# The beginning of a hybrid decoder step: modulation on four column tiles, square sums by a matrix of ones, three half weight tiles drawn forward

## The chip, the cores and the metric

One core of a Trainium2 chip. The metric is the device time of one launch in microseconds: 2328.43 us, the median of three runs (2324.95 to 2330.56). The profiled execution took 2327.78 us, of which 2326.1 us are the span that the profile shows.

## The reference

One layer of a decoder with two groups of heads beside each other, for a prompt of 2048 rows and for eight samples of four rows. Each row of width 1024 is normalised by its root mean square, scaled and shifted by a modulation that comes from a small vector `c`, and projected by one wide matrix. The projected columns feed a state-space group (Mamba-2, 16 heads) and a gated delta-rule group (8 heads), each behind a causal convolution of four taps; their outputs are joined, projected back, gated and added to the row.

```python
mod = jax.nn.silu(c.astype(f32)) @ w_ada.astype(f32) + b_ada.astype(f32)
shift, scale, gate = jnp.split(mod, 3, axis=-1)
h = _rmsnorm(x, norm_w) * (1.0 + scale[:, None]) + shift[:, None]
proj = h @ w_in.astype(f32)
z_s, xbc_raw, dt_raw, z_g, qkv_raw, a_raw, b_raw = _split(proj, IN_SIZES)
...
out = x.astype(f32) + gate[:, None] * (mix @ w_out.astype(f32))
```

The prompt and the eight samples have nine vectors `c`, so the modulation is a product of 9 rows with a 1024 x 3072 matrix.

## The kernel before

**Stages.** Stage one works on the prompt in four pieces of 512 rows. A piece's h is kept with the model dimension on partitions, as eight blocks (index k) of 128 x 512, split in a high and a low part (`hhi`, `hlo`); every product with `w_in` is three matmuls (high x high, low x high, high x low). Stage two, from 1859 us on, is the output projection. This study is about the beginning, in which the first piece's h is made.

**Making the first h.** `stat_first` (L290 to L303) loads the eight x blocks, squares each on ACT and sums the squares over partitions with matmuls against a column of ones, so that the sums stand with rows on partitions. `stat_row` takes the inverse root, writes it on a diagonal (L280) and spreads it over all partitions with a matmul by ones (L283). `h_load` multiplies x by it on DVE (L309); `h_make` applies scale and shift and casts to the high part on ACT (L313, L314) and forms the low part on DVE (L315).

**Modulation.** `ada_cols` (L161 to L175) makes 512 columns of the modulation, called a block here: four loads of 512 KB, eight fp32 matmuls of 9 x 512 (L168), a copy to SBUF (L170), four small matmuls that turn the rows into columns (L173, called the turn), and the bias on DVE (L174). There are two shift blocks and two scale blocks; blocks with index 0 serve k = 0 to 3, those with index 1 serve k = 4 to 7. `ada_gate` does the two blocks of the output gate at the end of stage one, two k at a time, in between other work (L195).

**The order.** PE's instructions stand as the Python code issues them. The code registers functions with a place `tau` (`at`) and runs them sorted by it; DVE, ACT, POOL and SP are ordered by a scheduler. Ahead of the sorted list run the first shift block, the square sums, the first scale block and the first four k of h. At `tau` 2.3 `second_half` runs the other two blocks and the other four k.

**Weight tiles.** A 128-column tile of `w_in` is used in two halves of four k, 12 matmuls each (L531), called first half and second half. `q0` opens a PSUM bank of the pool `ip` (three banks) and runs the first half, `q1` runs the second half and then the convolution of the result: a scaling on ACT (L536), three taps on DVE (L539, L545), a copy of the last columns on ACT (L547), a tanh on ACT (L548), a product on DVE (L549) that reads the bank last. `want` loads the halves ahead in the order of the list `halves` and splits them: a cast on ACT (L495), a subtraction on POOL (L496). Tiles 0, 1, 2, 3 below are the first four tiles.

**The decay gates.** `gates` multiplies h by a small matrix (L414, first for k = 0 to 3, then for k = 4 to 7), copies, turns it with four matmuls (L424), and `gate_set` computes softplus and decay on DVE and ACT (L343 to L366; the logarithm at L351 needs another function table of ACT than the tanh). Its last result `g_ln` goes to a cumulative sum on PE (L371, L372), and all heads need that.

## Time and profile before

| | |
|---|---|
| median of the runs | 2328.43 us |
| the profiled execution | 2327.78 us |
| its span | 2326.1 us |
| first matmul | 9.02 us |
| square sums end | 30.4 us |
| first matmul on h | 49.07 us |
| first matmul on the second half of h | 75.81 us |
| cumulative sum of the gates (L371) | 97.72 us |

A row of the timeline has the start in us, the duration in us, the engine, the line of the kernel, the operation with its output and inputs, the shapes, and how many instructions were merged (x4). In square brackets stands the idle time of the engine just before it and what released it. A matmul on plain fp32 leaves two records, one on the rounded fp32r type one. Rows of stretches give start:end, length, and the busy time of each engine with its number of instructions.

### The profile page before, as it was taken

Reading aid. Unit: us, or ns where it says so; the run is one execution under the profiler, and the core shown is the slowest. Engines: PE = TensorE matmul, PEld = TensorE weight load, DVE = VectorE, ACT = ScalarE, POOL = GpSimd, SP = SyncE. Lnnn points to the kernel's source line nnn. Section 1 sums busy time; section 2 is a strip of 40 time slices with the busy share of each in tenths; the row PEclk is TensorE's granted clock in tenths of the full one; section 3 lists DMA queues with packets and bytes.
Section 4 is the critical chain, followed back from the end, with each engine's and each line's share of the span. In section 5 each row is a group of like instructions: output and inputs, shape, how many; then the busy total and the mean of one; then the engine's idle time right before and its main releaser. Section 6 shows DMA issues by size and latency. Waiting matters only on the chain. (4 is left out here: it accounts for less than half of the span.)

```text
span 2326.1 us, 41856 instructions
## 1 busy us (share of the span) xinstructions
PE 2200.8 (95%) x15405; PEld 1864.9 (80%) x15405; DVE 1481.9 (64%) x3574; ACT 953.1 (41%) x2680; POOL 826.7 (36%) x1052
## 2 busy tenths in 40 slices
PE   6999999989999999999999989999999799998998
PEld 3688878868897887889788889998899377786786
DVE  2466868786767768675666776668676564454323
ACT  2534556454536445442533453435433432231111
POOL 3255665554437243411522241215211554322000
PEclk8999999999999999999999999999999999999999
DMA  6354655555766675465645544555445563643321
GB/s 239 113 167 152 191 166 180 181 181 174 225 214 209 213 225 183 143 193 165 191 153 179 178 135 132 180 154 157 150 147 160 165 211 125 191 155 128 129 86 52
DMA packets 241112, 387.94 MB, mean 167 GB/s; under 512 B 75880, under 2 KB 132968, under 8 KB 240908
## 3 DMA queue, kind: packets, MB, share of 16 engines
q1 hardware_dynamic: 240908, 385.28, 52.2%
q8 instruction: 121, 1.98, 0.3%
q14 instruction: 83, 0.68, 0.1%
HBM read 289.89 MB, written 95.30 MB: 166 GB/s over the span
## 5 line engine op out<-in xcount | busy, mean ns | idle before, releaser
L531 PE MATMUL pip<-hhi,w 128*128 128x512 f32 (+1 forms) x2880 | 823.7, 362 | 6.7 <-DVE kT L549 4.9
L531 PEld LDWEIGHTS pip<-hhi,w 128*128 128x128 f32 x2880 | 515.0, 190 | 85.0 <-issue 6.9
L531 PE MATMUL pip<-hlo,w 128*128 128x512 f32 (+1 forms) x1440 | 509.8, 354 | 0.0
L619 PE MATMUL pip<-w,hhi 128*128 128x256 f32 x2048 | 382.6, 287 | 0.3 <-DVE cv L549 0.3
L496 POOL TENSOR_TENSOR w<-xin,w 128x512 fp32r<-128x512 f32 x156 | 202.6, 1301 | 378.3 <-ACT w L495 344.8
L619 PEld LDWEIGHTS pip<-w,hhi 128*128 128x128 f32 x2048 | 316.5, 190 | 2.4 <-DVE cv L549 0.5
L531 PEld LDWEIGHTS pip<-hlo,w 128*128 128x128 f32 x1440 | 274.5, 191 | 36.9 <-issue 4.5
L619 PE MATMUL pip<-w,hlo 128*128 128x256 f32 x1024 | 289.4, 283 | 0.0
L1185 PE MATMUL pip<-wohi,mh 128*128 128x512 f32 x480 | 195.3, 407 | 7.4 <-ACT mh L1169 7.2
L619 PEld LDWEIGHTS pip<-w,hlo 128*128 128x128 f32 x1024 | 194.8, 190 | 0.0
L1185 PE MATMUL pip<-wohi,ml 128*128 128x512 f32 x480 | 189.7, 395 | 1.1 <-DVE ml L1176 1.0
L1185 PE MATMUL pip<-wolo,mh 128*128 128x512 f32 x480 | 189.1, 394 | 0.8 <-DVE wolo L238 0.8
L539 DVE SCALAR_TENSOR_TENSOR tr<-pip,cw,tr 128x509 f32<-128x509 f32 (+5 forms) x240 | 152.8, 637 | 40.2 <-ACT tr L536 37.1
L539 DVE SCALAR_TENSOR_TENSOR cv<-pip,cw,cv 128x509 f32<-128x509 f32 (+2 forms) x180 | 114.7, 637 | 44.6 <-ACT cv L536 42.5
L1000 POOL TENSOR_TENSOR L<-L,g_gc 128x512 f32<-128x512 f32 x64 | 70.9, 1120 | 198.4 <-DMA L<-rowsd 198.1
L495 ACT CAST w<-xin 128x512 fp32r<-128x512 f32 x156 | 95.1, 612 | 80.9 <-PE pip L619 25.9
L795 DVE TENSOR_TENSOR tl<-dl,ul 128x60 f32<-128x60 f32 (+21 forms) x432 | 121.0, 280 | 9.3
L797 DVE TENSOR_TENSOR dl<-dl,tl 128x60 f32<-128x60 f32 (+21 forms) x432 | 119.1, 276 | 9.0
L1185 PEld LDWEIGHTS pip<-wohi,mh 128*128 128x128 f32 x480 | 91.4, 190 | 27.0 <-ACT mh L1169 7.8
L1185 PEld LDWEIGHTS pip<-wohi,ml 128*128 128x128 f32 x480 | 91.0, 190 | 22.8 <-DVE ml L1176 3.0
L1185 PEld LDWEIGHTS pip<-wolo,mh 128*128 128x128 f32 x480 | 91.4, 190 | 18.2 <-DVE wolo L238 1.1
L1169 ACT CAST mh<-pch 128x512 fp32r<-128x512 f32 (+1 forms) x60 | 33.7, 562 | 166.4 <-PE pch L1166 166.3
(433 smaller groups left out, 4141.3 us busy)
## 6 DMA issues: line engine op xcount, KB each, us to landing
w<-wsp SPq DMA_DIRECT2D x260, 512.0 KB
wsp<-w SPq DMA_DIRECT2D x104, 512.0 KB
xin<-in_w_in SPq DMA_DIRECT2D x156, 256.0 KB
L<-rowsd SPq DMA_DIRECT2D x64, 256.0 KB
mx<-mixd SPq DMA_DIRECT2D x28, 512.0 KB
E<-rowsd SPq DMA_DIRECT2D x32, 256.0 KB
ul<-ud SPq DMA_DIRECT2D x64, 128.0 KB
mixd<-z SPq DMA_DIRECT2D x16, 512.0 KB
```

Source lines behind the costliest of these rows:

```text
L495: mark("ACT", s.copy(hi, rv))
L496: mark("POOL", g.tensor_tensor(lo, rv, hi, ALU.subtract))
L531: pe.matmul(pp, a[:, k, :], b[:, kk, cols], start=(i == 0), stop=(i == 23))
L539: v.scalar_tensor_tensor(u[:, c0 + dd:c0 + w], pp[:, 0:w - dd], cw[:, ci, k:k + 1], u[:, c0 + dd:c0 + w], ALU.mult, ALU.add)
L619: pe.matmul(out.rearrange("p (t c) -> p t c", t=2), a[:, k, cols], ws[b][:, :, k % 2, :], start=(first and k == 0 and e == 0), stop=(k == ...
L795: v.tensor_tensor(tmp[:, 0:r, 0:w], _bc(dl[:, 0:r, m], [P, r, w]), ul[:, m, m + 1:32].unsqueeze(1).to_broadcast([P, r, w]), ALU.mult)
L797: v.tensor_tensor(dl[:, 0:r, m + 1:32], dl[:, 0:r, m + 1:32], tmp[:, 0:r, 0:w], ALU.add)
L1000: g.tensor_tensor(L[:], L[:], _bc(G()["gc"][:, gi * 8 + q * 4:gi * 8 + q * 4 + 4, c], [P, 4, P]), ALU.subtract)
L1169: s.copy(mh[:, :, 0:n], ptv)
L1185: pe.matmul(pos[hb][0:m, :], a[:, k, 0:m], b[q * 4 + k][:, hb * 512:(hb + 1) * 512], start=(q == 0 and k == 0 and j == 0), stop=(q == 3 an ...
```

## The change

The first squares go through a full matrix of ones instead of a column, so that each k is one matmul of 512 columns; since the sums then stand along the free axis on every partition, a product with the identity and a reduction on DVE take the diagonal out. The square sums come ahead of the first shift block, in PE's order and in the loads.

The modulation's matmuls write to four column tiles: `sc` is padded to 32 columns, block k goes to PSUM partitions 32 (k mod 4) on. `sel`, four identities of 32 above each other, adds the four parts up in the turn. In `ada_gate` the bank is copied to SBUF and summed by an additional matmul with `sel`.

All eight x blocks are multiplied by the inverse root before the first four h are made. The second shift block stands at `tau` 0.9, the second scale block and the other h at 1.1; the first halves of the first three tiles stand at 1, 1.2 and 1.4, and their second halves at 5, 6 and 7. The later steps of the gates stand at 4.9, 6.4, 9 and 10.3 (before: 2.5, 4.1, 8.3, 10.3).

```diff
+    sc = keep.tile([P, KD, 32], F32, name="sc")
+    g.memset(sc[:], 0.0)
...
+    sel = keep.tile([P, 32], F32, name="sel")
+    for q in range(0, P, 32):
+        v.tensor_copy(sel[q:q + 32], ident[q:q + 32, q:q + 32])
+
+    def ada_mm(pa, k, w):
+
+        q = 32 * (k % 4)
+        pe.matmul(pa[q:q + 32, :], sc[:, k, :], w, start=(k < 4), stop=(k >= 4))
...
-            pe.matmul(pa[0:9, :], sc[:, k, :], raw[:, k % 2, :], start=(k == 0), stop=(k == KD - 1))
-        rowt = mk(trp, [P, T], "tr")[0:9]
-        s.copy(rowt, pa[0:9, :])
+            ada_mm(pa, k, raw[:, k % 2, :])
+        rowt = mk(trp, [P, T], "tr")
+        s.copy(rowt[:], pa[:])
         pt = psum("o")
         for k in range(4):
-            pe.transpose(pt[:, k * 9:(k + 1) * 9], rowt[:, k * P:(k + 1) * P], ident[0:9, 0:9])
+            pe.matmul(pt[:, k * 9:(k + 1) * 9], rowt[:, k * P:(k + 1) * P], sel[:, 0:9], start=True, stop=True)
...
-                pe.matmul(pa[0][0:9, :], sc[:, k, :], raw[:], start=(k == 0), stop=(k == KD - 1))
+                ada_mm(pa[0], k, raw[:])
             if k0 == KD - 2:
+                pq = mk(trp, [P, T], "tr")
+                s.copy(pq[:], pa[0][:])
+                pa[0] = psum("ip")
+                pe.matmul(pa[0][0:32, :], sel[:], pq[:], start=True, stop=True)
...
-            for c in range(NC):
-                pe.matmul(pr[:, c:c + 1], sq_[:, c * P:(c + 1) * P], ones[:, 0:1], start=(k == 0 and c == 0),
-                          stop=(k == KD - 1), skip_group_check=True)
+            pe.matmul(pr[:], ones[:], sq_, start=(k == 0), stop=(k == KD - 1))
+
+        dg = mk(trp, [P, T], "tr")[:].rearrange("p (c t) -> p c t", c=NC)
+        v.tensor_tensor(dg, pr[:].rearrange("p (c t) -> p c t", c=NC), ident.unsqueeze(1).to_broadcast([P, NC, P]),
+                        ALU.mult)
         stats[0] = mk(b1, [P, NC], "xss")
-        v.tensor_copy(stats[0][:], pr[:, 0:NC])
+        v.tensor_reduce(stats[0][:], dg, axis=mybir.AxisListType.X, op=ALU.add)
...
-        for i, t in enumerate((0, 1, 2.9, 7.3, 9.3) if p else (0, 2.5, 4.1, 8.3, 10.3)):
+        for i, t in enumerate((0, 1, 2.9, 7.3, 9.3) if p else (0, 4.9, 6.4, 9, 10.3)):
...
+            if p == 0 and pr == 0 and i < 3:
+
+                conv_tile(1 + 0.2 * i, n, p, ci, hc, dst, so + 3 + i)
+            else:
+                conv_tile(so + 2 * i, n, p, ci, hc, dst)
...
+    at(0.9, lambda: ada_shift(1))
+    at(1.1, lambda: ada_scale(1))
+    for k in range(4, KD):
+        at(1.1, lambda k=k: h_make(0, k))
...
+        stat_first()
         ada_shift(0)
-        stat_first()
         for _ in stat_row(0):
             pass
         ada_scale(0)
         load_wg()
+        for k in range(KD):
+            h_load(0, k)
         for k in range(4):
-            h_load(0, k)
             h_make(0, k)
```

Where the instructions stand now, at three places. SP's queue at the start, before (modulation weights from L167, x from L296):

```order
L91 DMA rw<-in_rows 128x64
L167 DMA kT_170<-in_w_ada 128x2x512
L167 DMA vs_174<-in_w_ada 128x2x512
L167 DMA qd_178<-in_w_ada 128x2x512
L167 DMA kd_182<-in_w_ada 128x2x512
L296 DMA cv_195<-in_x_pT 128x512
L296 DMA cv_203<-in_x_pT 128x512
```

and now (x from L308, modulation weights from L178):

```order
L91 DMA rw<-in_rows 128x64
L308 DMA cv_173<-in_x_pT 128x512
L308 DMA cv_178<-in_x_pT 128x512
L308 DMA cv_183<-in_x_pT 128x512
...
L308 DMA xdt_208<-in_x_pT 128x512
L178 DMA kT_218<-in_w_ada 128x2x512
L178 DMA vs_222<-in_w_ada 128x2x512
```

The eight x blocks moved ahead of the four loads of the first shift block.

PE's order from the gates' turn to the cumulative sum, before (pip_482, pip_560 and pip_605 are the banks of tiles 1, 2 and 3; each name with another weight buffer is one half; a half's further matmuls are left out):

```order
L424 MATMUL pbk_495<-id_136,sq_320 128x32 x4
L531 MATMUL pip_482<-hhi,w_353 128x512
...
L531 MATMUL pip_560<-hhi,w_449 128x512
...
L531 MATMUL pip_560<-hhi,w_475 128x512
...
L531 MATMUL pip_605<-hhi,w_527 128x512
...
L371 MATMUL pbk_618<-g_ln_525,cs 128x96
```

and now (pip_446 and pip_586 are tiles 2 and 3):

```order
L438 MATMUL pbk_522<-sel,sq_305 128x32 x4
L547 MATMUL pip_446<-hhi,w_439 128x512
...
L547 MATMUL pip_586<-hhi,w_468 128x512
...
L385 MATMUL pbk_599<-g_ln_552,cs 128x96
```

Four halves stood between the two, and now two: the second half of tile 2 and the first half of tile 3.

DVE's last steps up to `g_ln`, before (tr_544 is the convolution of tile 1):

```order
L356 TENSOR_TENSOR g_w_508<-g_w_508,g_au_513 128x96
L357 RECIPROCAL g_w_508<-g_w_508 128x96
L539 SCALAR_TENSOR_TENSOR tr_544<-pip_482,cw,tr_544 128x509
L358 TENSOR_TENSOR g_ln_510<-g_ln_510,g_w_508 128x96
L539 SCALAR_TENSOR_TENSOR tr_544<-pip_482,cw,tr_544 128x510
L359 TENSOR_TENSOR g_e_506<-g_e_506,g_ln_510 128x96
L539 SCALAR_TENSOR_TENSOR tr_544<-pip_482,cw,tr_544 128x511
L361 SCALAR_TENSOR_TENSOR g_sp_520<-g_u_502,g_e_506 128x96
L545 TENSOR_TENSOR tr_544<-tr_544,hc_331 128x3
L366 TENSOR_TENSOR g_ln_525<-g_sp_520,nega 128x96
```

and now (tr_513 is tile 1, kT_485 with pip_446 tile 2):

```order
L565 SCALAR_TENSOR_TENSOR tr_513<-pip_426,tr_513 128x512
L555 SCALAR_TENSOR_TENSOR kT_485<-pip_446,cw,kT_485 128x511
L369 TENSOR_TENSOR g_ln_537<-g_ln_537,g_au_540 128x96
L370 TENSOR_TENSOR g_w_535<-g_w_535,g_au_540 128x96
L561 TENSOR_TENSOR kT_485<-kT_485,hc_341 128x3
L371 RECIPROCAL g_w_535<-g_w_535 128x96
L565 SCALAR_TENSOR_TENSOR kT_485<-pip_446,kT_485 128x512
L372 TENSOR_TENSOR g_ln_537<-g_ln_537,g_w_535 128x96
L373 TENSOR_TENSOR g_e_533<-g_e_533,g_ln_537 128x96
L375 SCALAR_TENSOR_TENSOR g_sp_547<-g_u_529,g_e_533 128x96
L380 TENSOR_TENSOR g_ln_552<-g_sp_547,nega 128x96
```

The whole convolution of tile 2 and the closing product of tile 1 (L565, which waits for a tanh on ACT) now stand ahead of `g_ln`.

More of the change, by code (lines that the diff above doesn't have):

```diff
@@ L149, in hold @@
             yield
-    th9 = keep.tile([P, KD, 9], F32, name="th9")
-    sc = keep.tile([P, KD, 9], F32, name="sc")
-    s.activation(th9[:], ct[:], AF.Tanh, scale=0.5)
-    v.tensor_scalar(sc[:], ct[:], 0.5, None, ALU.mult)
-    v.scalar_tensor_tensor(sc[:], th9[:], 1.0, sc[:], ALU.add, ALU.mult)
+    th9 = mk(trp, [P, T], "tr")[:, 0:KD * 9].rearrange("p (k c) -> p k c", c=9)
+    sc = keep.tile([P, KD, 32], F32, name="sc")
+    g.memset(sc[:], 0.0)
+    s.activation(th9, ct[:], AF.Tanh, scale=0.5)
+    v.tensor_scalar(ct[:], ct[:], 0.5, None, ALU.mult)
+    v.scalar_tensor_tensor(sc[:, :, 0:9], th9, 1.0, ct[:], ALU.add, ALU.mult)
+    sel = keep.tile([P, 32], F32, name="sel")
[4 more added lines that the diff above has]
+        pe.matmul(pa[q:q + 32, :], sc[:, k, :], w, start=(k < 4), stop=(k >= 4))
     ADA = ("kT", "vs", "qd", "kd", "A", "U")
@@ L207, in hymba_step_kernel @@
     wg2 = keep.tile([P, KD, 64], F32R, name="wg2")
-    id2 = keep.tile([64, 32], F32, name="id2")
-    for q in (0, 32):
-        v.tensor_copy(id2[q:q + 32], ident[q:q + 32, q:q + 32])
     halo = keep.tile([P, NT, 3], F32, name="halo")
@@ L423, in gates @@
         for c in range(NC):
-            pe.matmul(pt[:, c * 32:(c + 1) * 32], gr[:, c * P:(c + 1) * P], id2[:], start=True, stop=True)
+            pe.matmul(pt[:, c * 32:(c + 1) * 32], gr[:, c * P:(c + 1) * P], sel[0:64], start=True, stop=True)
         if p == SP:
-            pe.matmul(pt[0:NS, 128:160], grs, id2[:], start=True, stop=True)
+            pe.matmul(pt[0:NS, 128:160], grs, sel[0:64], start=True, stop=True)
         raw = mk(b1, [P, NC + 1, 32], "g_raw")
@@ L520, in fill, with conv_tile @@
         return d
-    def conv_tile(tau, n, p, ci, hc, dst):
-        d = fill(tau, [(n, 0, False), (n, 1, False)])
+    def conv_tile(tau, n, p, ci, hc, dst, tau1=None):
+        d = {}
+        tau1 = tau + 1 if tau1 is None else tau1
+        ds = (fill(tau, [(n, 0, False)]), fill(tau1, [(n, 1, False)]))
         def mm(pp, hf, cols, i):
-            hi, lo = wt[d["i0"] + hf]
+            hi, lo = wt[ds[hf]["i0"]]
             for k in range(4):
@@ L551, in q0 @@
         def q0():
-            want(d["i0"])
+            want(ds[0]["i0"])
             d["pp"] = pp = psum("ip")
@@ L566, in q1 @@
             if p != SP:
-                want(d["i0"] + 1)
+                want(ds[1]["i0"])
                 mm(d["pp"][:], 1, slice(0, T), 12)
@@ L581, in conv_tile @@
         at(tau, q0)
-        at(tau + 1, q1)
+        at(tau1, q1)
     def z_pair(tau, n, p, mcol, done):
@@ L656, in gdn_pair @@
         for i, (n, ci, hc, dst) in enumerate(tiles_):
-            conv_tile(so + 2 * i, n, p, ci, hc, dst)
+            if p == 0 and pr == 0 and i < 3:
+                conv_tile(1 + 0.2 * i, n, p, ci, hc, dst, so + 3 + i)
+            else:
+                conv_tile(so + 2 * i, n, p, ci, hc, dst)
         def e_load(b):
@@ L1107, in hymba_step_kernel @@
             at(end + 1.5 + 8 * j + 2 * i, lambda part=part, i=i: part(2 * i))
-    def second_half():
-        ada_shift(1)
-        ada_scale(1)
-        for k in range(4, KD):
-            h_load(0, k)
-            h_make(0, k)
-    at(2.3, second_half)
+    at(0.9, lambda: ada_shift(1))
+    at(1.1, lambda: ada_scale(1))
+    for k in range(4, KD):
+        at(1.1, lambda k=k: h_make(0, k))
     with tc.manual_schedule(engines={mybir.EngineType.PE}):
+        stat_first()
         ada_shift(0)
-        stat_first()
         for _ in stat_row(0):
@@ L1123, in hymba_step_kernel @@
         load_wg()
+        for k in range(KD):
+            h_load(0, k)
         for k in range(4):
-            h_load(0, k)
             h_make(0, k)
```

## The prediction

> **What bounds the kernel now.** I read the page's busy shares first, then a table by stretches of the beginning, then the timeline of that beginning row by row. The page:
>
> ```profile
> PE 2200.8 (95%) x15405; PEld 1864.9 (80%) x15405; DVE 1481.9 (64%) x3574; ACT 953.1 (41%) x2680; POOL 826.7 (36%) x1052
> ```
>
> PE is the bound, and its order is written by hand, so a PE wait removed is time saved as long as nothing later waits for something else. The stretches (start:end, length, busy us of PE, PEld, DVE, ACT, POOL; then granted clock, DMA share, GB/s):
>
> ```profile
> 9.00:31.00 22.00, 19.98 (x84) 13.04 (x84) 0.95 (x4) 6.83 (x12) 5.67 (x15) 0.80 1.05 387
> 31.00:49.00 18.00, 11.50 (x22) 2.39 (x22) 8.31 (x14) 5.81 (x10) 4.22 (x3) 0.78 0.58 206
> 49.00:84.00 35.00, 29.35 (x87) 12.72 (x88) 5.99 (x12) 10.13 (x18) 1.26 (x1) 0.85 0.06 22
> 84.00:98.00 14.00, 14.00 (x66) 11.26 (x65) 10.31 (x25) 8.44 (x17) 5.17 (x4) 1.00 0.44 145
> 98.00:126.00 28.00, 27.76 (x180) 24.75 (x179) 16.12 (x29) 18.33 (x60) 20.71 (x21) 1.00 0.44 149
> ```
>
> Up to 31 us DMA is the wall (387 GB/s); up to 84 us PE waits or runs below full clock; from 84 us it is full. The change lies before 98 us. Its rows (start, duration, [idle before <- releaser]):
>
> ```profile
> 5.16 0.23 DVE L156 SCALAR_TENSOR_TENSOR sc<-th,sc 128x72 f32<-128x72 f32 x1
> 9.02 3.23 PE L168 MATMUL pbk<-kT,sc 128*9 128x512 f32 x4 [9.02 <-DMA kT<-in_w_ada]
> 12.09 1.88 PE L168 MATMUL pbk<-vs,sc 128*9 128x512 f32 x4
> 13.65 0.63 ACT L298 ACTIVATE L<-cv 128x512 f32<-128x512 f32 x1 [6.20 <-DMA cv<-in_x_pT]
> 17.70 0.63 ACT L298 ACTIVATE L<-xD 128x512 f32<-128x512 f32 x1 [0.70 <-DMA xD<-in_x_pT]
> 24.18 0.40 ACT L237 CAST wg<-xin 128x256 fp32r<-128x256 f32 x1 [2.33 <-DMA xin<-in_w_gate]
> 28.60 1.84 PE L300 MATMUL pbk<-ones,E 128*128 128x1 f32 x8
> 30.48 0.16 DVE L303 COPY xss<-pbk 128x4 f32<-128x4 f32 x1 [5.45 <-PE pbk L300]
> 32.92 2.07 PE L283 MATMUL pbk<-E,ones 128*128 128x512 f32 x2 [2.47 <-DVE E L280]
> 35.65 5.84 DVE L309 TENSOR_TENSOR cv<-cv,sq 128x512 f32<-128x512 f32 x6 [2.78 <-ACT sq L285]
> 42.01 0.68 DVE L309 TENSOR_TENSOR xdt<-xdt,sq 128x512 f32<-128x512 f32 x1
> 45.35 0.20 DVE L183 SCALAR_TENSOR_TENSOR s<-s,vec 128x36 f32<-128x36 f32 x1
> 49.07 0.50 PE L414 MATMUL pbk<-hhi,wg 128*64 128x512 f32 x1 [3.98 <-ACT hhi L314]
> ```
>
> Here the first h is ready at 49.07, held up by the square sums, which end at 30.4.
>
> **To the first h.** The x tiles now stand ahead of the first 2.1 MB of modulation weights instead of behind them. At 387 GB/s that is 5.4 us: first x at 13.65 - 5.4 = 8.2, eighth at 17.70 + 0.68 (one more such tile) - 5.4 = 13.0. The sums become eight fp32 matmuls of 512 columns. The row of four records at 9.02 is two such matmuls on the cold clock (1.6 us each), the one at 12.09 two warm (0.86 each, with the next row's start 1.7 later). From 8.2 + 0.65 (square), two cold and six warm end at 17.2; the bound is two more cold ones, 18.7. The wider `sc` and `sel` cost nothing: `sc` was ready at 5.4, and the x tiles cover it.
>
> From there to the first x product took 35.65 - 30.48 = 5.2 us. The diagonal is now a 512-wide multiply and a reduce: no row shows the reduce; between the 0.16 copy and the 0.97 of L309's costliest rows for each step, I take 0.65 twice, +1.2. L283 gets a warm clock: -1.0 (bound 0). That gives 22.6. The shift block now stands ahead of L283 on PE: its last weights land where the eighth x did (17.70 + 0.68 = 18.4), and half a block, a copy and a turn (0.9 + 0.6 + 1.1, priced below) end at 21.0, just when the diagonal is ready (17.2 + 32.92 - 30.48 + 1.2 = 20.8). Products start near 23. All eight now come before the first scale and shift: 5.84 + the last two were 7.0; six of those rows ran beside POOL's weight splits, the last start 0.6 apart; POOL is idle now, so 5.0 (up to 7.0): 28.0. Behind them in DVE's order stand the gate weights' low part and the two small scale steps, 0.9: 28.9. The scale block isn't late: the gate weights landed at 24.18 with the same bytes ahead of them, so its last tile lands at 23.8. From L183's end (45.55) to the first h took 3.5 us. So the first gate matmul moves from 49.07 to 32.4: **16.7 us gained**.
>
> On SP's queue the first two weight tiles (0.5 MB) now stand behind the second shift block and ahead of the second scale block. From 24.2 they land by 24.2 + 2.6 MB / 387 GB/s = 31, and the scale block (2.1 MB more) by 36.4; PE asks for them at 40 and 43 (below), so this costs nothing. If DMA were a third slower, the scale block would come at 42.5, still in time.
>
> **From the first h to tile 3.** One block is one column group of modulation (eight matmuls):
>
> ```profile
> 55.68 1.89 PE L168 MATMUL pbk<-qd,sc 128*9 128x512 f32 x4
> 60.84 1.88 PE L168 MATMUL pbk<-U,sc 128*9 128x512 f32 x4
> 62.75 0.57 ACT L170 COPY tr<-pbk 9x512 f32<-9x512 f32 x1 [6.30 <-PE pbk L168]
> 63.38 0.41 PE L173 MATMUL po<-cs,tr 9*128 9x9 f32 x4 [0.67 <-ACT tr L170]
> 75.81 0.69 PE L414 MATMUL pbk<-hhi,wg 128*64 128x512 f32 x1 [3.98 <-ACT hhi L314]
> 80.27 0.63 PE L531 MATMUL pip<-hhi,w 128*128 128x512 f32 x2
> 85.47 1.07 PE L424 MATMUL pbk<-id,sq 64*128 64x32 f32 x8
> 97.72 0.35 PE L371 MATMUL pbk<-g_ln,cs 128*128 128x96 f32 x2
> 98.08 0.48 PE L531 MATMUL pip<-hhi,w 128*128 128x512 f32 x1
> 2084.36 1.06 PE L1499 MATMUL po<-L,gr 128*32 128x512 f32 x8
> ```
>
> A block takes 62.7 - 55.7 = 7.0 us. The last row is eight records, four fp32 matmuls of the same width, on four column tiles: 1.06 us, where two rows like that at 55.68 are 3.6. Two such rounds, the second 0.86 behind, make a block of 1.9 us. The Trainium skill (TensorE: Matmul & The Clock Gate, Part 3) gives 2.38x for three column tiles; by that the block would be 2.9 us, and with two on the path the result 2 us later. The row has 3.4x and is this kernel's own.
>
> The four small matmuls that turn the block's rows into columns (0.41) now contract 128 partitions like L424 (1.07). A turn with its copy thus costs PE 1.9 us; half a weight tile is 12 matmuls at 0.23, 2.8 us. In order from 32.4: gates 3.9 (3.35 before, two weight casts now between the h casts), shift block 0.4 + 1.9, turn 1.9, tile 0 first half 2.8, scale block 2.3, turn 1.9, tiles 1 and 2 first halves 5.6, gates 1.8 (the last h is ready by then, so the wait of 3.98 at 75.81 goes), tile 0 second half 2.8: 25.3, to 57.7. For colder blocks I add 0.5, with 3.4 as the bound.
>
> **A new wait** follows. The gates' cumulative sum (L371, now L385) comes two tile halves after the gates' turn instead of four, and its input passes DVE and ACT in order behind three convolutions:
>
> ```profile
> 82.78 0.78 ACT L536 ACTIVATE kT<-pip,cb,cw 128x512 f32<-128x512 f32 x1 [2.38 <-PE pip L531]
> 88.34 1.28 ACT L351 ACT_TABLE_LOAD   x1
> 89.64 0.28 ACT L351 ACTIVATE g_ln<-g_w 128x96 f32<-128x96 f32 x1
> 94.84 0.26 DVE L366 TENSOR_TENSOR g_ln<-g_sp,nega 128x96 f32<-128x96 f32 x1
> 94.95 1.28 ACT L548 ACT_TABLE_LOAD   x1 [0.69 <-DVE tr L545]
> 96.25 0.60 ACT L548 ACTIVATE pip<-tr 128x512 f32<-128x512 f32 x1
> 96.88 0.69 DVE L549 SCALAR_TENSOR_TENSOR tr<-pip,tr 128x512 f32<-128x512 f32 x1 [1.79 <-ACT pip L548]
> ```
>
> Before, g_ln was ready (95.1) when PE came (97.72). Now, from the end of tile 2: ACT's scaling 0.2 + 0.78, a weight cast 0.6, a halo copy 0.2, table load 1.28, Ln 0.28, load 1.28, tanh 0.60: 5.2. The load and tanh of tile 1 stand ahead on DVE of the rest: L549 0.69, a tap 0.7, four small steps 1.3, L549 of tile 2 0.69, and the last four gate steps 1.4: 4.8. g_ln comes 10.0 us after tile 2. PE has only tile 3's first half (2.8) and, ahead of it, a 0.7 us wait for a PSUM bank, as three open halves hold all three. So PE stands 6.5 us; behind it are tile 3's second half and everything else. Bounds 4.5 and 8.5. Then it runs cold:
>
> ```profile
> 125.38 0.39 PE L749 MATMUL pbk<-tr,kT 128*128 128x128 f32 x2
> 128.32 0.77 PE L748 MATMUL pbk<-kT 128*128 128x128 f32 x2 [2.56 <-DVE A L755]
> ```
>
> A wait of 2.56 us doubles a pair's time; after the one of 3.98 half clock lasted from 75.81 to 80.0. I put 2.0.
>
> Tile 3's second half, which began at 98.08, begins effectively at 57.7 + 0.5 + tile 1, turn, tile 2 (6.7) + 0.7 + 2.8 + 6.5 + 0.4 + 2.0 = 77.3. **Gain 20.8 us.** After that the orders are alike.
>
> **The end of stage one.** The gate's modulation:
>
> ```profile
> L195 PE MATMUL pip<-xin,sc 128*9 128x512 f32 x32 | 16.0, 620 | 1.3 <-DMA xin<-in_w_ada 1.3
> ```
>
> Eight pairs at 1.9 become about 1.0 (two tiles side by side), -7; two new sums of a copy and a full matmul cost PE 1.8 each, +3.6, and sit ahead of the recurrence's own steps. That stretch is a chain of PE, DVE and ACT in turn, so I put 0, between -3 and +3.
>
> **The sum.** The profiled execution took 2327.78 us (span 2326.1), 0.65 below the median 2328.43. 2327.8 - 20.8 = 2307.0 by its own time, 2307.5 against the median. With +-2 at the products, 3 at the clock, 2 at the wait and 3 at the end not all on one side, this case's own range is 2301 to 2314.
>
> **Rivals.**
> - *No new wait* at the cumulative sum, because DVE and ACT get through sooner: 6.5 + 2.0 less, 2299. For it: DVE is 74% busy from 84 to 98, not full. Against: the two table loads in one chain. Chance 0.14.
> - *A longer wait* (10 us and more): 2314 to 2318. Chance 0.05.
> - *The column tiles don't overlap*, so the change doesn't do what it says: 5 us for each of the two blocks on the path and 6.6 at the scale, 2324. L1499's row speaks against it. 0.05.
> - *The lead is lost later*, to something not paced by PE: 2328. The stretch from 98 to 126 has PE at 27.76 of 28 us, with DMA share at 0.44, so nothing seems to pace it. 0.05.
> - *Half clock* through the new, patchier beginning: slower. Each us of PE work at half clock costs 0.5 us of it again, so 42 us of work kept at half clock take the whole lead, and 50 make 2332 or more, beyond 0.2%. Between 9 and 49 us the clock did average 0.8, but beside the one-column matmuls of L300, which go. 0.04.
>
> The forecast itself has 0.67. A measurement here tells about 0.2% from no change. Faster: 0.67 + 0.14 + 0.05 = 0.86; the same: tiles that don't overlap and the lost lead, 0.10; slower 0.04. The range 2297 to 2318 takes in the missing wait and the longer one.
>
> **What would show it.** Right: x landing near 8, sums over near 17, the first gate matmul near 32, blocks near 1.9 us, an idle of 4.5 to 8.5 us on PE before L385 with DVE's g_ln as releaser, tile 3's second half at 73 to 81. Wrong: blocks of 7 us; no idle at L385; a lead of 20 us there that is smaller at 200 or at 1800 us; square sums that end after 22.

## The result and the profile after

The changed kernel takes 2312.43 us (median of four runs, 2308.60 to 2317.61), the kernel before 2328.90: ratio 0.9933, 95% interval 0.9910 to 0.9956. That is 16.5 us less; 20.8 were forecast, and 2312.4 lies in the range. The two profiled executions differ by more: span 2306.9 instead of 2326.1, 19.2 us less; but the one profiled after the change is the fastest of its four runs, so this flatters the change. Measured once more in a later group, beside other runs of the kernel before, the ratio is 0.9907 (0.9892 to 0.9921).

The page of the changed kernel, the busy shares:

```profile
PE 2173.7 (94%) x15377; PEld 1853.1 (80%) x15377; DVE 1482.5 (64%) x3577; ACT 953.9 (41%) x2682; POOL 823.0 (36%) x1053
```

PE is busy 27.1 us less, more than the time that was gained: some of what went was work at half clock, and some idle time came in its place. The same stretches as before the change, of the changed kernel (start:end, length, busy us of PE, PEld, DVE, ACT, POOL; granted clock, DMA share, GB/s):

```profile
9.00:31.00 22.00, 15.18 (x66) 6.37 (x64) 8.16 (x19) 8.05 (x14) 4.39 (x14) 0.96 1.05 385
31.00:49.00 18.00, 14.82 (x71) 6.84 (x72) 4.97 (x7) 6.29 (x12) 6.85 (x5) 0.76 0.64 214
49.00:84.00 35.00, 27.11 (x114) 20.50 (x113) 18.84 (x39) 18.89 (x38) 8.46 (x7) 0.90 0.33 110
```

DMA is busy up to 31 us as before. But the eight x products now lie there (DVE 8.16 instead of 0.95 us), and more of the weight tiles' convolutions fall between 49 and 84 us (DVE 18.84 instead of 5.99). The clock column must be read with care at the start: it reads 1.00 until its first recorded change, though the rows below show the first sums at half the pace of the later ones. Rows picked from the timeline of the changed kernel up to the first gate matmul (start, duration, [idle before <- releaser]):

```profile
7.96 2.05 PE L311 MATMUL pbk<-L,ones 128*128 128x512 f32 x2 [7.96 <-ACT L L310]
16.21 1.02 PE L311 MATMUL pbk<-E,ones 128*128 128x512 f32 x2
17.27 0.69 DVE L314 TENSOR_TENSOR tr<-pbk,cs 128x512 f32<-128x512 f32 x1 [10.17 <-PE pbk L311]
...
20.95 1.12 PE L295 MATMUL pbk<-E,ones 128*128 128x512 f32 x2
22.73 3.70 DVE L323 TENSOR_TENSOR cv<-cv,sq 128x512 f32<-128x512 f32 x6 [1.62 <-ACT sq L297]
28.11 0.20 DVE L194 SCALAR_TENSOR_TENSOR s<-s,vec 128x36 f32<-128x36 f32 x1
31.83 0.69 PE L428 MATMUL pbk<-hhi,wg 128*64 128x512 f32 x1 [6.13 <-ACT hhi L328]
```

The sums end at 17.2 us (30.5 before), the x products start at 22.7 (35.7), s is ready at 28.3 (45.6), and the first gate matmul stands at 31.83 (49.07). Then the parts behind it, picked from the same timeline:

```profile
31.81 1.29 DVE L329 TENSOR_TENSOR hlo<-cv,hhi 128x512 fp32r<-128x512 f32 x2 [3.50 <-ACT hhi L328]
32.89 3.03 POOL L510 TENSOR_TENSOR w<-xin,w 128x512 fp32r<-128x512 f32 x2 [12.91 <-ACT w L509]
33.37 3.11 DVE L329 TENSOR_TENSOR hlo<-cv,hhi 128x512 fp32r<-128x512 f32 x2 [0.27 <-ACT hhi L328]
37.15 1.07 PE L166 MATMUL pbk<-qd,sc 128*32 128x512 f32 x2
39.68 0.60 PE L166 MATMUL pbk<-U,sc 128*32 128x512 f32 x2
44.87 0.62 PE L166 MATMUL pbk<-kT,sc 128*32 128x512 f32 x2
46.19 0.60 PE L166 MATMUL pbk<-kd,sc 128*32 128x512 f32 x2
54.06 0.39 PE L428 MATMUL pbk<-hhi,wg 128*64 128x512 f32 x1
55.18 1.48 POOL L510 TENSOR_TENSOR w<-xin,w 128x512 fp32r<-128x512 f32 x1 [0.20 <-PE pbk L428]
55.45 1.76 DVE L329 TENSOR_TENSOR hlo<-xdt,hhi 128x512 fp32r<-128x512 f32 x1
57.26 0.45 PE L428 MATMUL pbk<-hlo,wg 128*64 128x512 f32 x1 [1.00 <-DVE hlo L329]
63.21 1.07 PE L438 MATMUL pbk<-sel,sq 64*128 64x32 f32 x8
76.59 0.26 DVE L380 TENSOR_TENSOR g_ln<-g_sp,nega 128x96 f32<-128x96 f32 x1
77.00 0.71 PE L385 MATMUL pbk<-g_ln,cs 128*128 128x96 f32 x2 [6.29 <-DVE g_ln L380]
77.84 0.77 PE L547 MATMUL pip<-hhi,w 128*128 128x512 f32 x1
109.33 0.46 PE L768 MATMUL pbk<-kT 128*128 128x128 f32 x2 [2.54 <-DVE A L775]
```

The scale block runs from 44.87 to 46.8: 1.9 us, as forecast. The shift block took 3.1 (37.15 to 40.28), at half clock. The new wait is there, 6.29 us at L385 with g_ln as its releaser, and tile 3's second half starts at 77.84 (98.08 before).

The last row is a landmark that every kernel below has: the first wait for A in the recurrence's set-up, 128.32 us before the change. Its start tells what the beginning is worth: **19.0 us** here. Between two profiles of the same kernel it moved by 1.6 us (the first experiment), so differences below that say nothing. The time of a whole run tells it less well, as the table at the end of the experiments shows.

### The profile page after: what moved, and what is told of

It reads as the page before. It is cut to its first block, busy times and chain, and to the rows that moved or that the text cites. A ratio compares the mean times of both kernels' runs of the same rounds, so it can differ in the third digit from the quotient of the medians.

```text
span 2306.9 us, 41800 instructions
## 1 busy us (share of the span) xinstructions
PE 2173.7 (94%) x15377; PEld 1853.1 (80%) x15377; DVE 1482.5 (64%) x3577; ACT 953.9 (41%) x2682; POOL 823.0 (36%) x1053
```

## The experiments

They ran in four groups, each on one chip beside runs of the kernel before, which took 2334 to 2336 us there (2329 in the comparison above). So ratios are compared, and starts of rows; the landmark's start in each kernel's timeline stands in the table at the end. The kernel before has one profile only, from the comparison above.

**The changed kernel again** (no edit).

> The changed kernel itself, once more, so that the runs of this group are compared on one chip. Every theory: first gate matmul between 31.4 and 32.6 us, the wait at L385 between 6 and 6.6 us, 0.993 of the time before. Where the two chips differ, the lead of other kernels over the first profile of the changed kernel drifts by some us between 1000 and 1800 us, and this run drifts with them; if the drift belongs to the edits, this run shows none.

Measured: 2312.04 us, 0.9907 of the 2335.92 of its group. The wait at L385 is 6.3 us again. The first gate matmul stands at 32.73, 0.1 later than expected, and the landmark at 110.89, 1.6 us later than in the first profile: between executions the beginning varies by at least this much. 0.9 us of it is there at the sums, of which one more runs at the slow pace (they end at 18.1 instead of 17.2). The first matmul of stage two stands at 1844.72 us here and at 1839.87 in the first profile, with no edit between them, so drifts of a few us in later rows say nothing of an edit.

**The loads' order alone.**

```diff
+        stat_first()
         ada_shift(0)
-        stat_first()
```

> The kernel before with one change: the first eight x tiles are loaded and squared ahead of the first modulation block; sums by columns, one column tile, the old order of the rest. Theory A, the loads' order alone is worth the part of the first step that does not come from shorter blocks: square sums end near 17.5 us, first gate matmul at 38.5 to 41 us (49.07 before), tile 3's second half at 88 to 91 us (98.08 before), time 0.995 to 0.998 of before. Rival B, the blocks of 7 us now stand in the chain where the loads stood, and little is gained: first gate matmul after 44 us, time within 0.002 of before.

Measured: 2332.04 us, ratio 0.9983 (0.9969 to 0.9997). Timeline:

```profile
20.15 1.84 PE L300 MATMUL pbk<-ones,E 128*128 128x1 f32 x8
44.74 0.69 PE L414 MATMUL pbk<-hhi,wg 128*64 128x512 f32 x1 [3.98 <-ACT hhi L314]
```

x lands as in the changed kernel, yet the landmark comes only 3.9 us sooner than before, where A expected 7 to 10 (at tile 3's second half): the sums by columns end at 22.0 us, not 17.5, and blocks of 7 us stand behind them. The first gate matmul after 44 us and a ratio within 0.002 are rival B's. The order of the loads makes room, and little else.

**Sums by columns in the changed kernel.**

```diff
-            pe.matmul(pr[:], ones[:], sq_, start=(k == 0), stop=(k == KD - 1))
+            for c in range(NC):
+                pe.matmul(pr[:, c:c + 1], sq_[:, c * P:(c + 1) * P], ones[:, 0:1], start=(k == 0 and c == 0),
+                          stop=(k == KD - 1), skip_group_check=True)
...
-        v.tensor_reduce(stats[0][:], dg, axis=mybir.AxisListType.X, op=ALU.add)
+        v.tensor_copy(stats[0][:], pr[:, 0:NC])
```

> The changed kernel with the first square sums made as before, by four matmuls of one column for each x tile, and copied; loads first, column tiles and pulled halves stay. From the run with the loads alone: a tile's sums take 1.71 us there instead of 0.86, so the eight end at 22.0 us instead of 17.2, and the diagonal's multiply and reduce (1.2 us) are saved. Theory A, sums by ones are a term of their own, 4 to 5 us less what the diagonal costs: first gate matmul 3 to 5 us later than 31.8 us, the same at tile 3's second half, 2314 to 2318 us where the changed kernel has 2312. Rival B, the scale block's weights or the blocks set the time there and the sums are hidden: first gate matmul less than 1.5 us later.

Measured: 2326.79 us, ratio 0.9980 (0.9963 to 0.9996).

```profile
20.10 1.84 PE L312 MATMUL pbk<-ones,E 128*128 128x1 f32 x8
40.59 0.69 PE L427 MATMUL pbk<-hhi,wg 128*64 128x512 f32 x1 [7.98 <-ACT hhi L327]
```

The landmark is 6.1 us later than in the changed kernel's second run. A is right in kind and its term too small: the first gate matmul is 7.9 us later than in that run, where 3 to 5 were expected. The sums end 3.8 us later (21.94 against 18.13; 17.23 in the first profile), and the shift block behind them runs at half clock, so that the x products start 5.0 us later. GpSimd's first weight splits then fall beside them: six take 5.84 us here and 3.70 in the changed kernel, and the scale step s takes 1.1 more. By the ratios the time is 17 us above the changed kernel's, more than the beginning explains.

**Column tiles alone**, in the kernel before.

```diff
-            pe.matmul(pa[0:9, :], sc[:, k, :], raw[:, k % 2, :], start=(k == 0), stop=(k == KD - 1))
+            q = 32 * (k % 4)
+            pe.matmul(pa[q:q + 32, :], sc[:, k, :], raw[:, k % 2, :], start=(k < 4), stop=(k >= 4))
...
-            pe.transpose(pt[:, k * 9:(k + 1) * 9], rowt[:, k * P:(k + 1) * P], ident[0:9, 0:9])
+            pe.matmul(pt[:, k * 9:(k + 1) * 9], rowt[:, k * P:(k + 1) * P], sel[:, 0:9], start=True, stop=True)
```

> The kernel before with column tiles in the four modulation blocks of the beginning (and the full turns) alone; loads, column sums, order of the weight tiles and the end of stage one as before. Theory A, of the 17.5 us that column tiles are worth inside the change, the two second blocks bring 2 x 5.1 less 2 x 0.65 for the turns, 8.9 us, wherever they stand, and the two first ones less than there, 2 to 5 us, because loads and column sums hold the beginning up: first gate matmul at 44 to 47 us (49.07 before), tile 3's second half at 84 to 87 us (98.08 before), 0.994 to 0.996 of before. Rival B, the terms simply add: tile 3's second half near 80.5 us. Rival C, without the earlier loads the overlap is hidden: later than 90 us.

Measured: 2326.78 us, ratio 0.9972 (0.9959 to 0.9985). A row of the table by stretches, then the timeline:

```profile
18.40:28.70 10.30, 10.30 (x50) 10.22 (x49) 0.42 (x1) 3.15 (x6) 2.49 (x2) 0.50 1.05 386
```

```profile
16.61 1.03 PE L302 MATMUL pbk<-ones,L 128*128 128x1 f32 x8
26.86 1.85 PE L302 MATMUL pbk<-ones,E 128*128 128x1 f32 x8
43.33 0.69 PE L416 MATMUL pbk<-hhi,wg 128*64 128x512 f32 x1 [5.31 <-ACT hhi L316]
```

The landmark is 13.6 us sooner than before, and tile 3's second half stands at 84.42, within A's 84 to 87; the first gate matmul is 0.7 us sooner than A's 44 to 47, and the ratio is a smaller gain than A's. Only 5.7 us of the lead is there at the first gate matmul; the rest comes from the two second blocks. And the rows show the price of the sums by columns: the sums of the first x tile took 1.03 us, behind a modulation block that had kept PE warm. Then, with PE at work for all of 10.30 us, the granted clock is 0.50 and a tile's sums take 1.85.

**One column tile in the changed kernel.**

```diff
-        q = 32 * (k % 4)
-        pe.matmul(pa[q:q + 32, :], sc[:, k, :], w, start=(k < 4), stop=(k >= 4))
+        pe.matmul(pa[0:32, :], sc[:, k, :], w, start=(k == 0), stop=(k == KD - 1))
...
-        s.copy(rowt[:], pa[:])
+        s.copy(rowt, pa[0:32])
...
```

> The four modulation blocks of the beginning accumulate all eight matmuls on one column tile (rows 0 to 31), copy and turn 32 rows; the end of stage one keeps its four column tiles. Theory A, the overlap of column tiles is worth 5.1 us a block, all four on the path: blocks of 7.0 us, the first gate matmul near 40 us instead of 31.8, tile 3's second half 15 to 18 us later than the 77.8 us of the changed kernel, time 2325 to 2331 us. Rival B, much of it lies beside other work (x products on VectorE, the wait at L385): the second half of tile 3 less than 10 us later.

Measured: 2333.40 us, ratio 0.9999 (0.9987 to 1.0011): nothing is left of the gain.

```profile
40.48 0.69 PE L428 MATMUL pbk<-hhi,wg 128*64 128x512 f32 x1 [3.98 <-ACT hhi L328]
94.36 0.74 PE L385 MATMUL pbk<-g_ln,cs 128*128 128x96 f32 x2 [6.19 <-DVE g_ln L380]
```

Theory A in the rows: the first gate matmul at 40.5, the cumulative sum 17.4 us later, the landmark 18.0 later than in the first profile (16.4 than in the second). The wait at L385 is 6.19 us again: it follows the gates' turn, wherever that stands (from the turn to the sum 13.7 us here, 13.8 in both profiles of the changed kernel).

**No pulled halves.**

```diff
-            if p == 0 and pr == 0 and i < 3:
-
-                conv_tile(1 + 0.2 * i, n, p, ci, hc, dst, so + 3 + i)
-            else:
-                conv_tile(so + 2 * i, n, p, ci, hc, dst)
+            conv_tile(so + 2 * i, n, p, ci, hc, dst)
...
-        for i, t in enumerate((0, 1, 2.9, 7.3, 9.3) if p else (0, 4.9, 6.4, 9, 10.3)):
+        for i, t in enumerate((0, 1, 2.9, 7.3, 9.3) if p else (0, 2.5, 4.1, 8.3, 10.3)):
...
-    at(0.9, lambda: ada_shift(1))
-    at(1.1, lambda: ada_scale(1))
+    at(2.3, lambda: ada_shift(1))
+    at(2.3, lambda: ada_scale(1))
     for k in range(4, KD):
-        at(1.1, lambda k=k: h_make(0, k))
+        at(2.3, lambda k=k: h_make(0, k))
```

> The first halves of the weight tiles 1 and 2 go back behind the modulation, and the gates' steps and the second modulation blocks to their places of before (both blocks one behind the other after tile 0's first half); loads first, sums by ones and column tiles stay. Theory A, the pulled halves fill a wait of about 4 us ahead of the second gate matmuls but make the wait at L385: without them PE stands 3.5 to 5 us at L428 and under 0.5 us at L385, tile 3's second half starts at 75.5 to 77.5, that is 0.5 to 2.5 us sooner than with them, and the run is 0 to 3 us faster than the changed kernel. Rival B, the pulled halves are a real part of the gain: tile 3's second half 3 us or more later than 77.8.

Measured: 2317.98 us, ratio 0.9930 (0.9913 to 0.9946).

```profile
60.54 1.07 PE L438 MATMUL pbk<-sel,sq 64*128 64x32 f32 x8
72.80 0.35 PE L385 MATMUL pbk<-g_ln,cs 128*128 128x96 f32 x2
```

The sum stands at 72.80 with no wait ahead of it: four weight-tile halves lie between the gates' turn (60.54) and it, 12.3 us of work, and g_ln is ready by then. PE stands 4.0 us ahead of the second gates instead. The landmark, at 103.39, comes 5.9 us sooner than in the first profile of the changed kernel, 7.5 sooner than in the second: A, by more than it expected. In the beginning the pulled halves cost time. But A's 0 to 3 us in the time aren't there: the ratio is 0.9930, and the changed kernel's two are 0.9933 and 0.9907, so that the times can't be told apart, and the profiled span (2315.3) is 6 to 8 us longer. The lead goes in the middle of the run: the gates' turn of the next 512 tokens (L438) stands at 472.51 here and at 470.34 in the changed kernel's second run, 2.2 us later. One stretch of this kernel, then of that run:

```profile
455.00:465.00 10.00, 5.22 (x22) 2.71 (x20) 8.40 (x18) 6.58 (x17) 2.27 (x2) 0.86 0.45 124
```

```profile
455.00:465.00 10.00, 7.25 (x33) 4.19 (x32) 9.60 (x15) 7.21 (x18) 6.30 (x6) 0.83 0.79 225
```

PE does 2.0 us less here, at the step to the next 512 tokens, with VectorE at 84% and 96%; from 435 to 445 us it does 2.7 less (7.30 and 10.00). The order of execution differs too: the scheduler sets the order on every engine but PE, and after the edit VectorE makes a low part of the next tokens' h (L329) elsewhere among the steps of the recurrence. Whether that order or the clock takes the lead was not tried; it stays open.

**The cumulative sum later.**

```diff
-        for i, t in enumerate((0, 1, 2.9, 7.3, 9.3) if p else (0, 4.9, 6.4, 9, 10.3)):
+        for i, t in enumerate((0, 1, 2.9, 7.3, 9.3) if p else (0, 4.9, 6.4, 10.2, 10.9)):
```

> The gates' cumulative sum (L385) and its transpose (L406) stand two events later on TensorE: behind the second half of weight tile 3, the four turns of q and the first half of weight tile 4 (6.2 us of matmuls at full clock more ahead of it); all else is the changed kernel. Theory A, the wait of 6.3 us at L385 is time of the whole kernel: the wait falls below 1.5 us, the matmuls behind it no longer run at half clock, L406 comes 6 to 8 us sooner than the 85.2 us of the changed kernel, the lead is still there at 300 us, and the run is 4 to 9 us faster than the changed kernel (about 2304 us). Rival B, VectorE and ScalarE pace the stretch up to the first recurrence, so that what is saved here is waited for at L768 or L706: the lead against the changed kernel at 130 us is below 2 us.

Measured: 2314.82 us, ratio 0.9914 (0.9899 to 0.9928).

```profile
79.14 0.46 PE L385 MATMUL pbk<-g_ln,cs 128*128 128x96 f32 x2 [1.17 <-DVE g_ln L380]
81.22 0.29 PE L406 MATMUL pbk<-cs,g_gc 128*96 128x128 f32 x1 [0.96 <-DVE g_gc L389]
```

The wait is 1.17 us, with 0.96 more at L406. The landmark is 4.4 us sooner than in the first profile, 5.9 than in the second. Up to there the wait at L385 was real time, as A says, and 2.1 us of it came back at the two places; L406 stands 4.0 us sooner than the 85.2, not A's 6 to 8. But A's 4 to 9 us in the time aren't there: the ratio lies within the interval of the changed kernel's, and the profiled span (2314.6) is longer than both of its spans (2306.9 and 2308.8). What takes the lead back wasn't found.

**No table loads in the first gates.**

```diff
-        s.activation(ln, w, AF.Ln)
+        s.activation(ln, w, AF.Tanh if first else AF.Ln)
...
```

> In the first gate set alone the logarithm is computed as a tanh, so that ScalarE loads no other table before it and none behind it (the softplus of the first 512 tokens is another number). Theory A, the two table loads of 1.28 us lie in the chain that feeds the cumulative sum (VectorE stood 1.17 and 0.93 us behind them): the wait at L385 falls from 6.3 to between 3.5 and 4.5 us. Rival B, VectorE's in-order queue of convolution steps sets the time by itself and the loads are hidden beside it: the wait stays above 5.5 us.

Measured: one run of 2316.66 us. The row of the waits (total, times, longest), then two of the timeline:

```profile
PE pbk L385 <- DVE g_ln L380: 5.0, 1, 5.0
```

```profile
71.78 1.30 POOL L510 TENSOR_TENSOR w<-xin,w 128x512 fp32r<-128x512 f32 x1 [2.69 <-ACT halo L563]
72.14 1.00 DVE L366 TENSOR_SCALAR g_w<-g_w 128x96 f32<-128x96 f32 x1
```

5.0 us lies between the two theories. In the changed kernel VectorE stood idle 1.17 us ahead of L366 for the logarithm, and L366 then took 0.21; here it doesn't wait, but takes 1.00, and ends 0.06 us after a weight split on GpSimd. From the copy of the gates' turn (L442) to g_ln VectorE shows no idle time here. So taking out the loads is worth 1.3 of the 6.3 us; the rest is VectorE's queue, in which the gates' steps stand between the convolutions of three tiles. Part of that queue is GpSimd: in the changed kernel L357 takes 0.91 and L369 0.69, each ending 0.12 us after a split, where steps of the same shape without a split take 0.26. The landmark (111.09) doesn't show the 1.3, since the turn of the shift block and tile 0's first half ran at half clock in this execution (that turn takes 1.88 instead of 1.06).

**One half pulled instead of two.**

```diff
-            if p == 0 and pr == 0 and i < 3:
+            if p == 0 and pr == 0 and i < 2:
...
-        for i, t in enumerate((0, 1, 2.9, 7.3, 9.3) if p else (0, 4.9, 6.4, 9, 10.3)):
+        for i, t in enumerate((0, 1, 2.9, 7.3, 9.3) if p else (0, 4.9, 5.5, 8.3, 10.3)):
...
-    at(0.9, lambda: ada_shift(1))
+    at(1.05, lambda: ada_shift(1))
```

> Only tile 1's first half stays pulled; tile 0's first half stands ahead of both second modulation blocks and tile 1's behind them, tile 2 goes back to its old place, the gates' turn stands ahead of tile 1's second half and the cumulative sum behind tile 3's first half, so that four halves (11.2 us) lie between the two instead of two. Theory A, the cover of the gates' chain is counted in weight-tile halves between turn and sum: the wait at L385 falls from 6.3 to under 1.5 us, and one half (2.8 us) still fills the wait ahead of the second gates: tile 3's second half starts at 66 to 70 us instead of 77.8, and the run is 6 to 11 us faster than the changed kernel of this group. Rival B, DVE and ACT pace the stretch whatever PE's order: L385 still waits over 3 us or L768 takes it back, and the lead at 130 us is under 4 us.

Measured: 2308.42 us, ratio 0.9892 (0.9876 to 0.9909). Timeline:

```profile
25.95 3.44 POOL L510 TENSOR_TENSOR w<-xin,w 128x512 fp32r<-128x512 f32 x2 [5.19 <-ACT w L509]
28.20 1.75 DVE L323 TENSOR_TENSOR xD<-xD,sq 128x512 f32<-128x512 f32 x1
34.74 0.69 PE L428 MATMUL pbk<-hhi,wg 128*64 128x512 f32 x1 [8.27 <-ACT hhi L328]
76.62 0.43 PE L385 MATMUL pbk<-g_ln,cs 128*128 128x96 f32 x2 [3.18 <-DVE g_ln L380]
```

A was wrong on all its numbers: L385 waits 3.18 us (under 1.5 expected), tile 3's second half stands at 77.06 (66 to 70), and the landmark is 3.6 us sooner than in the changed kernel's second run, the time about as much, not 6 to 11. Rival B's numbers are there, a wait over 3 us and a lead under 4. Two things A had not counted: g_ln comes 15.9 us after the turn here, so that four halves don't cover it (without pulled halves four were enough), as convolutions and GpSimd's splits crowd VectorE; and the first splits now run beside the x products, one of which takes 1.75 us where 0.68 is the rule, so that the first gate matmul is 2.0 us later than in that run (2.9 than in the first profile).

**Scale first, splits late, sum late.** Added to the last edit:

```diff
-        for i, t in enumerate((0, 1, 2.9, 7.3, 9.3) if p else (0, 4.9, 5.5, 8.3, 10.3)):
+        for i, t in enumerate((0, 1, 2.9, 7.3, 9.3) if p else (0, 4.9, 5.5, 9.05, 10.3)):
...
+        c = s.copy(hhi[:, k, 0:T], xk)
+        if p == 0 and k < 4:
+            first_h[0] = c.ins
...
+            with tc.issue_after(first_h[0]):
+                mark("ACT", s.copy(hi, rv))
...
+        s0 = ada_scale(0)
+        with tc.issue_after(s0.ins):
+            load_wg()
+        for k in range(KD):
+            if k < 4:
+                h_load(0, k)
+            else:
+                with tc.issue_after(s0.ins):
+                    h_load(0, k)
```

> The kernel with only tile 1's first half pulled, and three edits more: VectorE makes the scale s before the last four x products, the first weight splits stand behind the first four h casts on ScalarE (so that GpSimd's low parts no longer run beside the x products), and the cumulative sum stands behind tile 3's second half. Theory A, what held the first h were VectorE's queue and products that took 1.75 us beside GpSimd's splits instead of 0.68: s is ready at 25 to 27 us (28.3 in the changed kernel, 31.2 with one half pulled), the first gate matmul at 29 to 31 us, the wait at L385 under 1 us, the lead over the changed kernel 7 to 11 us at 130 us, time 4 to 9 us below the changed kernel. Rival B, the late splits hold tile 0 up by what is gained (PE waits over 2 us for its low part), or what is gained by 130 us is given back at the next position: time within 3 us of the changed kernel.

Measured: **2303.20 us, ratio 0.9878 (0.9857 to 0.9899)**, the lowest of all.

```profile
26.25 0.20 DVE L194 SCALAR_TENSOR_TENSOR s<-s,vec 128x36 f32<-128x36 f32 x1
29.97 0.69 PE L431 MATMUL pbk<-hhi,wg 128*64 128x512 f32 x1 [3.98 <-ACT hhi L329]
71.78 0.43 PE L388 MATMUL pbk<-g_ln,cs 128*128 128x96 f32 x2 [0.45 <-DVE g_ln L383]
```

A on every number: s at 26.5, the product of 1.75 us at 0.68 again, the first gate matmul at 30.0, 0.45 us of wait, the landmark (99.92) 11.0 us sooner than in the changed kernel's second run, and a time 7 us lower by the ratios. The interval overlaps that run's at its edge (0.9892 to 0.9899), and those of one half pulled (0.9892) and of two edits alone (0.9887) by more, so that the times of these three can't be told apart.

**Two of these edits alone**, on the changed kernel: `s` first and the late splits.

> The changed kernel with two of the last run's edits alone: VectorE makes the scale s before the last four x products, and the first weight splits stand behind the first four h casts on ScalarE. TensorE's order is the changed kernel's, with both halves pulled and the sum at its place. Theory A, of the 11 us by which the last run led the changed kernel at 130 us these two bring 3 to 6, by an earlier first h and by low parts of h that no longer run beside GpSimd (gates of 3.4 to 4 us instead of 5.3): first gate matmul at 29.5 to 30.5 us, and since the wait at L385 follows from the gates' turn it stays at 5.5 to 6.5 us and the lead of 3 to 6 us is there at 130 us. Rival B, the second blocks' weights or tile 0's low part then hold TensorE up: lead under 2 us at 130 us. Rival C, most of the last run's lead is here: over 7 us.

Measured: 2309.03 us, ratio 0.9887 (0.9871 to 0.9904).

```profile
31.47 0.69 PE L431 MATMUL pbk<-hhi,wg 128*64 128x512 f32 x1 [3.99 <-ACT hhi L329]
35.37 0.82 PE L166 MATMUL pbk<-qd,sc 128*32 128x512 f32 x2
```

The gates take 3.9 us (31.47 to 35.37), as was forecast for the change itself, instead of 5.3, and L385 waits 6.3 us, as A says. The landmark is 3.2 us sooner than in the changed kernel's second run: A at its lower end, with a first gate matmul that comes 1 us late. The other 8 us of the last kernel are left for the halves' order (3.6 by itself) and the late sum, which was not measured alone in that order.

**The end of stage one undone.**

```diff
-                ada_mm(pa[0], k, raw[:])
+                pe.matmul(pa[0][0:9, :], sc[:, k, 0:9], raw[:], start=(k == 0), stop=(k == KD - 1))
...
-                pq = mk(trp, [P, T], "tr")
-                s.copy(pq[:], pa[0][:])
-                pa[0] = psum("ip")
-                pe.matmul(pa[0][0:32, :], sel[:], pq[:], start=True, stop=True)
```

> Only the end of stage one is put back: the gate's modulation accumulates on one column tile of 9 columns, without the two copies and sums (L209, L211); the beginning is the changed kernel's. Theory A, pairs of 1.9 us and sums with their waits cancel: the lead over the changed kernel between 1760 and 1850 us changes by -2 to +2 us and the time is that of the changed kernel within its interval. Rival B, the two copies and their waits (2.7 us of idle time at L211) cost more than the column tiles give: 2 to 4 us faster. Rival C, the column tiles are worth their 7 us: 3 us or more slower.

Measured: 2313.27 us, ratio 0.9917 (0.9893 to 0.9941). The gate's modulation by line (busy us, mean ns | idle before, releaser), of this kernel between 1770 and 1860 us, then of the changed kernel's second run:

```profile
L206 PE MATMUL pip<-xin,sc 128*9 128x512 f32 x32 | 16.1, 623 | 1.3 <-DMA xin<-in_w_ada 1.3
```

```profile
L166 PE MATMUL pip<-xin,sc 128*32 128x512 f32 x32 | 9.9, 703 | 0.0
L211 PE MATMUL pip<-tr,sel 128*32 128x512 f32 x4 | 2.1, 605 | 1.4 <-ACT tr L209 1.4
```

The tiles save 6.2 us of PE and a wait of 1.3, and the two sums add 2.1 and 1.4 of wait. The last step of the recurrence ahead of all that (L909, here L905) stands at 1762.44 us with the column tiles and at 1763.55 without, the first matmul of stage two at 1844.72 and 1844.87: the stretch takes 82.3 us with them and 81.3 without. That is theory A, no more than 2 us; what the tiles save on PE is not time there.

**All of them beside each other** (the landmark's start, how much sooner than the 128.32 of before, how much shorter the same execution's span is than the 2326.1 of before, and the ratio of the times):

| kernel | landmark | sooner | span shorter by | ratio |
|---|---|---|---|---|
| changed | 109.33 | 19.0 | 19.2 | 0.9933 |
| changed, again | 110.89 | 17.4 | 17.3 | 0.9907 |
| loads alone | 124.46 | 3.9 | -3.8 | 0.9983 |
| tiles alone | 114.69 | 13.6 | 3.7 | 0.9972 |
| changed, column sums | 116.99 | 11.3 | 3.2 | 0.9980 |
| changed, one column tile | 127.31 | 1.0 | -2.3 | 0.9999 |
| changed, no pull | 103.39 | 24.9 | 10.8 | 0.9930 |
| changed, sum later | 104.96 | 23.4 | 11.5 | 0.9914 |
| changed, no table loads | 111.09 | 17.2 | 11.2 | one run |
| changed, end undone | 110.83 | 17.5 | 17.6 | 0.9917 |
| one half pulled | 107.33 | 21.0 | 18.6 | 0.9892 |
| two edits alone | 107.66 | 20.7 | 16.9 | 0.9887 |
| scale first | 99.92 | 28.4 | 22.9 | 0.9878 |

The parts come near the whole at the landmark: loads 3.9, tiles 13.6, sums by ones 6.1 (116.99 less 110.89), pulled halves -7.5 (103.39 less 110.89) make 16.1; 17.4 was measured. They are not independent, though: taken out of the changed kernel the column tiles are worth 16.4, put into the kernel before 13.6. The ends follow with less order. The changed kernel and the one with the end undone keep their lead to the end of the span; all others lose 2.3 us (one half pulled) to 14.1 us (no pull) of it. The ratios can't be laid beside these leads, since the kernel before took 2327.78 us in the profiled execution and 2334 to 2336 in the groups.

## Why the prediction was right

**To the first h** it was right part by part. The sums end at 17.2 (forecast 17.2), the diagonal's two steps take 0.69 each (0.65), L295 stands at 20.95 (21.0), the products start at 22.7 (near 23), s is ready at 28.3 (28.9), the first gate matmul comes 17.2 us sooner (16.7). Some of this is luck: x landed 1 us sooner than the 8.2 forecast (first square at 7.19), more than two of the sums ran at the slow pace, and the two errors cancel; in the second profile, with one more slow sum, the sums end at 18.1. What the prediction did not say is which part of the change earned it: x landing 6 us earlier is worth 3.9 us by itself; the sums by ones and the short blocks turn the early x into an early h.

**From the first h to tile 3** the blocks are 1.9 us at full clock, as L1499's row had it, and not the 2.9 by the Trainium skill's figure for three tiles (TensorE: Matmul & The Clock Gate, Part 3). Three sizes were off. The gates took 5.3 us instead of 3.9 and the second gates 3.6 instead of 1.8 (54.06 to 57.7), both because VectorE's low parts of h ran beside GpSimd's low parts of the weights: two took 1.29 us without them and the next two 3.11. The prediction had priced the casts between the h on ScalarE, not the operation behind them on GpSimd; it also took the last h to be ready, whose low part came at 57.2. With the splits out of the way the first gates took 3.9; for the second gates no run took the splits away. The shift block ran at half clock and took 3.1, 0.8 more than its 2.3, of which 0.5 was allowed for. In all L385 came 2.1 us later than the sum's terms say (77.0, where 77.3 less 0.4 less 2.0 is 74.9).

**The new wait** is right: 6.3 us (forecast 6.5), then 1.8 at half clock (forecast 2.0: the lead is 20.7 at L385 and 19.0 after tile 3's second half), and 0.4 for the bank (0.7). Its working named the two table loads and VectorE's queue, and counted both loads (2.56 us) in full; taking them out gave 1.3, since VectorE's queue then sets the time. It had no term for the steps that GpSimd's splits hold up in that queue. And the section costed only this wait, and never asked what the change would be without the pulled halves. It is better by 5.9 to 7.5 us up to the landmark: what the halves fill ahead of the second gates is less than what their place takes from the gates' chain.

**The end of stage one** is near 0, as put down (the stretch is 1.0 us longer with the column tiles than without), out of -7 and +3.6.

**The sum.** 20.8 us forecast, 19.0 at the landmark, 19.2 over the two profiled spans, 16.5 between the medians. The profiled execution (2308.60) is 1.6 us above the 2307.0 forecast against its own time; the median is 3.8 us above that execution. Of the rivals none came true: the wait neither stayed away nor grew to 10 us, the tiles overlap, and the lead was not lost as a whole: at stage two the first profile is 19.6 us ahead of the kernel before (1839.87 and 1859.47), the second 14.7. There is half clock in the beginning, but between 49 and 84 us less of it than before (0.90, before 0.85).

## What to carry to other kernels

Where a step is moved ahead to fill a wait, count what then remains between the producer and the consumer of every chain that it was covering; here two weight-tile halves ahead of the gates took 5.6 us from the cover of the gates' own chain. Price the second engine of each pair that is moved: the cast was cheap, and its partner on GpSimd slowed the operation on VectorE that the path needed. And judge an edit of the beginning by a row soon behind it, then by the time: without pulled halves the lead over the changed kernel was 7.5 us at the landmark, and at 470 us a lag of 2.2.
